# A hybrid decoder layer on one core: the SSM states' pool laid under the logarithms', conv tails turned in a bank of another ring, halves and norm products tied to other steps

## The chip, the cores and the metric

One core of a Trainium2 chip. The kernel is one launch; its time is the device time in microseconds of that launch, the median of several executions. A profile of one execution stands beside it, with its own time.

## The reference

One inference step of a hybrid decoder layer, for a prompt of 512 positions and for 8 samples of 8 new positions each, 576 columns in all, in fp32. D_MODEL is 1024.

```python
def trunk_layer(x, conv_prev, h0, past, p):
    h = x + 0.5 * swiglu(rmsnorm(x, p['ffn1_norm']), ...)          # d_ff 2816
    xn = rmsnorm(h, p['mix_norm'])
    z, xbc, dt_raw, q, k, v, f_raw, g_ssd, g_att = split_combined(xn @ p['w_in'])
    y_ssd, h_new, conv_new = ssd_branch(z, xbc, dt_raw, conv_prev, h0, p)
    q = rmsnorm(q...); k = rmsnorm(k...)                             # per head of 64
    logf = jax.nn.log_sigmoid(f_raw + p['b_f'])
    y_att = fox_attention(q, k_all, v_all, logf_all)                 # past: 2048 paged keys a sample
    merged = (jax.nn.sigmoid(g_ssd) * (y_ssd @ p['w_ssd_proj'])
              + jax.nn.sigmoid(g_att) * (y_att @ p['w_attn_proj']))
    h = h + merged @ p['w_out']
    return h + 0.5 * swiglu(rmsnorm(h, p['ffn2_norm']), ...), (k, v, logf, h_new, conv_new)

def ssd_branch(z, xbc, dt_raw, conv_prev, h0, p):
    xc, conv_new = causal_conv(xbc, conv_prev, ...)                  # 4 taps, SiLU; last 3 rows are an output
    xs, Bm, Cm = jnp.split(xc, ...)                                  # 32 heads of 64; 4 groups of B and C, 128 wide
    y, h_new = ssd_scan(xh, dt, A, Bm, Cm, h0)                       # chunks of 128
    yg = (y + d_skip * xh) * jax.nn.silu(z)
    return yg * lax.rsqrt(mean(yg * yg over a group) + eps) * p['ssd_norm'], h_new, conv_new
```

In a chunk of the scan, y is `(C B^T * decay) @ (x dt)` plus `C` times the state carried in; the state after a chunk is the decayed one plus `B^T` times the decayed `x dt`.

## The kernel before

Activations lie transposed: 128 features on the partitions, the 576 columns along the free axis, worked in two halves of 288. A weight tile of 128x512 comes by DMA from SyncE's queue into `stage`, is rounded by ScalarE into `whi` (L177), and VectorE or GpSimd writes the rest into `wlo` (L178). A product is then three matmuls a tile of 128: hi·hi, hi·lo, lo·hi (`mm3`, L212 to L214), over 128x288. These are called weight matmuls here; a conv tile has 48 of them, a piece of an output product 12.

The text is written for a scheduler (Tile): it fixes for each engine one order of instructions, from the text's order, from priorities (`soon()` puts a few steps ahead) and from ties. `behind(later, first)` is such a tie: it only says that one instruction must not stand before another. Tiles come from pools; a tag has a number of buffers (`bufs`) that are used in turn, and whoever takes one in the text waits until its last user in the text is done. PSUM, which matmuls write, has eight banks: rings of two named `tr`, `mm` and `pv`, and two of `acc`.

In order: the first feed-forward, with side work in between, advanced in steps by a generator (`aside`); the input projection; attention over the pages, with the z part of the projection between (`beside`); then the SSD branch, group by group; the gates, the output projection; the second feed-forward.

What the change touches:

- `aside` loads the rows of the conv state (pool `rows`), then the paged logarithms (pool `lg`): prefix sums, and 32 stores to `pastD` from ScalarE's queue. Then `turns` (pool `turn`, opened after `lg` is closed) loads the 32 tiles of the SSM state (`h`, 256 KB each), turns each with four transposes on TensorE (L390) into a bank `tr`, copies it out and stores it.
- `headnorm` and eight products with `sel8` (L815, two instructions each) spread the q norms' factors over the partitions for the samples; the matmuls of L702 and L786 stand by them. All use 24 partitions.
- In `beside`, a job of z ends with `v = (tanh(v) + 1) * v`, one instruction of VectorE (L1051), and a store to `zD`.
- `conv_tile` makes one of the six tiles of a group (B, C, four of x): two accumulators, moved to `xr` (three buffers, L1154 to L1161); the columns after the prompt are turned (L1167), copied to `tt` (L1169) and stored as outputs; four taps (`kf`, L1178 and L1180), tanh, product (L1182 and L1184). The turned tail goes into the free columns of the second accumulator's own bank, `full`.
- `group_scan(g)` works through the samples' chunk (c = 4) and then the chunks 0 to 3: `cb` (L1312), the log differences `ab` loaded by DMA (L1321), `dk` by ScalarE (relu L1326, exponent L1327) and VectorE (product L1328), x turned (L1337), `xdt` and `xde` (L1342, L1344), then `pv` (L1355, L1359) and the carry of the state (L1370). Samples' parts (`hT`, L1384; `oo`, L1394; L1404) and the last states (L1418, L1420) follow. `halves` writes the gated result in two parts, `ygh` and `ygl` (L1288, L1289).
- `group_in(g + 1)`, the next group's six conv tiles, stands in the text after `group_scan(g)`, and `group_out(g)`, the product with `w_ssd_proj`, after that. `rowscale` (L263 and L265, then small steps of VectorE) gives the norm's factor by which `group_out` scales its accumulators (L1443 to L1446); it takes a bank `tr`.
- The ring `acc` also gives each conv tile's accumulators: `convs` keeps instructions of each tile for ties.

```python
for g in range(4):
    cur = nxt
    *gated, lows = group_scan(g, *cur)
    if g < 3:
        nxt = group_in(g + 1)
        for x in lows[2:4]:
            behind(x, convs[6 * g + 6][3])
    for _ in range((3, 0, 0, 5)[g]):
        j = next(late)
        gate_tile(gs, j, 8 + j)
    if g < 3:
        group_out(g, *gated)
```

Of the kernel before, what the change touches and what calls it, by code (L numbers as in the profile page):

```python
# [23 lines left out]
P = 128  # L24
# [3 lines left out]
NS = 64  # L28
# [65 lines left out]
def build(ctx, tc, A, O):  # L94
# [8 lines left out]
    def pool(name, bufs=1, **kw):  # L103
        return tc.tile_pool(name=name, bufs=bufs, **kw)
# [103 lines left out]
    def mm3(out, w, xs, half, first=True, last=True):  # L208
        n = len(w)
        for i, ((hi, lo), (xh, xl)) in enumerate(zip(w, xs)):  # L210
            a, b = xh[:, hs(half)], xl[:, hs(half)]
            mm(out, lhsT=hi, rhs=a, start=first and i == 0, stop=False)  # L212
            mm(out, lhsT=hi, rhs=b, start=False, stop=False)  # L213
            mm(out, lhsT=lo, rhs=a, start=False, stop=last and i == n - 1)  # L214
# [159 lines left out]
    def turns(wait):  # L374

        for _ in range(wait):
            yield
        with pool("turn", side="right", reuse_waits="tile") as sp_:
            tiles = []
            for t in range(16):  # L380
                for h in range(2):
                    for n in range(len(tiles), min(2 * t + h + 3, 32)):
                        tiles.append(tl(sp_, [P, 4, P], tag="h0", bufs=4))
                        (nc.scalar if n < 3 else nc.sync).dma_start(out=tiles[n], in_=ap3(A["state_ssm"][0], *place(n % 2, n // 2)))
                    if t + h == 0:
                        yield
                    h0 = tiles[2 * t + h]
                    ps = tr()
                    for b in range(4):
                        nc.tensor.transpose(ps[:, b * P:(b + 1) * P], h0[:, b, :], ident)  # L390
                    hT = tl(sp_, [P, 512], tag="hT", bufs=3)
                    act(hT, ps, AF.Copy)
                    nc.scalar.dma_start(out=hTD[h, t], in_=hT)
                    yield

# [27 lines left out]
    with pool("h1", reuse_waits="tile") as hp:  # L423
# [98 lines left out]
        def aside():  # L522

            with pool("rows", side="right", reuse_waits="tile") as su:

                sc = tl(su, [24, CONV], tag="sc")
                for j in range(3):
                    nc.scalar.dma_start(out=sc[j * B:(j + 1) * B], in_=A["state_conv"][0, :, j, :])
                yield
                yield  # L530
                scT = tl(su, [P, 24, 24], tag="scT")
                for j in range(0, 24, 12):
                    t = tr()
                    for i in range(12):
                        nc.tensor.transpose(t[:, i * 24:(i + 1) * 24], sc[:, (j + i) * P:(j + i + 1) * P], ident[:24, :24])
                    V.tensor_copy(scT[:, j:j + 12, :], t[:, :288].rearrange("p (i c) -> p i c", c=24))
                nc.scalar.dma_start(out=scD, in_=scT)

            with pool("lg", side="right", reuse_waits="tile") as lp:
                pcol = tl(lp, [P, 1], I32, tag="pcol")  # L540
                nc.scalar.dma_start(out=pcol, in_=A["page_table"].rearrange("b n -> (b n)").unsqueeze(1))
                lg = tl(lp, [P, P, 16], tag="lg")
                G.indirect_dma_start(out=lg.rearrange("p s h -> p (s h)"), out_offset=None,
                                     in_=A["cache_logf"].rearrange("o n s h -> (o n) (s h)"),
                                     in_offset=bass.IndirectOffsetOnAxis(ap=pcol[:, :1], axis=0))
                pf = tl(lp, [P, 16, P], tag="pf")
                for h in range(16):
                    V.tensor_tensor_scan(pf[:, h, :], C("one"), lg[:, :, h], 0.0, ALU.mult, ALU.add)
                tot = tl(lp, [P, 16], tag="tot")
                V.tensor_copy(tot, pf[:, :, P - 1])  # L550
                page = tl(lp, [P, P], tag="page")
                nc.scalar.dma_start(out=page, in_=A["consts"][:, COFF["page"][0]:COFF["page"][0] + P])
                for _ in range(2):
                    yield
                t = sm()
                mm(t[:, :16], lhsT=page, rhs=tot, start=True, stop=True)
                st = tl(lp, [P, 16], tag="st")
                V.tensor_copy(st, t[:, :16])

                for h in range(16):  # L560
                    G.tensor_tensor(lg.rearrange("p s h -> p (s h)")[:, h * P:(h + 1) * P].rearrange("p (q r u) -> p r q u", q=4, u=4),
                                    pf[:, h, :].rearrange("p (r q u) -> p r q u", q=4, u=4),
                                    st[:, h:h + 1].unsqueeze(2).unsqueeze(3).to_broadcast([P, 8, 4, 4]), ALU.subtract)
                lv = lg.rearrange("p s h -> p (s h)").rearrange("p (h q e) -> p h q e", h=16, q=4)
                for b in range(B):
                    for q in range(4):
                        nc.scalar.dma_start(out=pastD[b, :, q].rearrange("h g e -> g h e"), in_=lv[b * NPG:(b + 1) * NPG, :, q, :])
            yield from turns(1)
# [92 lines left out]
    with pool("att", side="right", reuse_waits="tile") as ap:  # L661
# [147 lines left out]
        G.memset(qz, 0.0)  # L809
        t = sm()  # L810
        for j in range(8):
            sel = sel8[:, j].rearrange("k e m -> k (e m)")
            if j == 0:
                headnorm(qt[0], sel, 64)
            mm(t[:, j * NS:(j + 1) * NS], lhsT=sel, rhs=hr[:, NP:], start=True, stop=True)  # L815
# [211 lines left out]
        def beside():  # L1027
            jobs = [(ga, j) for j in range(8)] + [(zc, j) for j in range(16)]
            ahead = ga.get(0)
            for n, (cols, j) in enumerate(jobs):  # L1030
                w, ahead = ahead, None
                v = tl(mixp, [P, NT], tag="kf", bufs=2)
                for half in range(2):
                    a = acc()
                    for k in range(0, 8, 4):
                        mm3(a, w[k:k + 4], xs[k:k + 4], half, first=k == 0, last=k == 4)
                        if half == 0 and k == 0 and n + 1 < len(jobs):
                            ahead = jobs[n + 1][0].get(jobs[n + 1][1])
                        if k == 0:
                            yield  # L1040
                    with soon():
                        V.scalar_tensor_tensor(v[:, hs(half)], a, 0.5, rbc[:, hs(half)], ALU.mult, ALU.mult)
                    if half == 0:
                        yield
                if cols is ga:
                    act(v, v, AF.Tanh)
                    nc.scalar.dma_start(out=thD[:, j, :], in_=v)
                else:
                    th = tl(tp, [P, NT], tag="sq", bufs=1)
                    act(th, v, AF.Tanh)  # L1050
                    V.scalar_tensor_tensor(v, th, 1.0, v, ALU.add, ALU.mult)  # L1051
                    nc.scalar.dma_start(out=zD[:, j, :], in_=v)
                yield

        filler = beside()
# [26 lines left out]
        for _ in range(24):  # L1082
            fill()
        for n in range(2):
            keys_of(n)
# [58 lines left out]
    def conv_tile(ct, w, prev, out):  # L1144
# [10 lines left out]
        full = tl(accp, [P, 512], tag="acc")  # L1155
        a = full[:, :HT]
# [8 lines left out]
        with soon():  # L1165
            t = full[:n, 512 - P:]
            turned = nc.tensor.transpose(t, xr[:, NP:], ident)  # L1167
            tt = tl(xz, [n, P], tag="tt", bufs=1)
            act(tt, t, AF.Copy)  # L1169
# [37 lines left out]
    with qyp:  # L1207
        with pool("yhl", reuse_waits="tile") as yhp:

            yhl = []  # L1210
            for n, y in enumerate(yt):
# [4 lines left out]
                for x, first in zip((c, h, V.tensor_tensor(lo, y, hi.bitcast(F32), ALU.subtract)), convs[1 + n // 2]):  # L1216
                    behind(x, first)
# [27 lines left out]
    with pool("ssd", side="right", reuse_waits="tile") as wk:  # L1245
# [13 lines left out]
        def group_scan(g, bT, cT, xg):  # L1259
# [8 lines left out]
            yhl, lows, owns = [], [], []  # L1268
# [12 lines left out]
            def halves(half):  # L1281

                for i in range(4):
# [4 lines left out]
                    act(hi, xg[:, i, hs(half)], AF.Copy, scale=w)  # L1288
# [17 lines left out]
            def chunk(c, hst):  # L1306
# [6 lines left out]
                if c == 4:  # L1313
                    behind(cb, convs[6 * g + 2][4])
# [3 lines left out]
                for r0 in (0, 4):  # L1318
# [8 lines left out]
                    act(dv, dv, AF.Exp, scale=-1.0)  # L1327
                    V.tensor_tensor(dv, dv, cbm[:n, :n].unsqueeze(1).to_broadcast([n, 4, n]), ALU.mult)  # L1328
# [60 lines left out]
            for c in range(4):  # L1389
# [5 lines left out]
                if c == 2 and g < 3:  # L1395
                    halves(0)

# [32 lines left out]
            return ysq, yhl, lows  # L1430
# [31 lines left out]
        for g in range(4):  # L1462
            cur = nxt
            *gated, lows = group_scan(g, *cur)
# [90 lines left out]
```

## Time and profile before

| | |
|---|---|
| median of 3 runs | 1868.68 us (1864.07 to 1872.83) |
| profiled execution | 1873.55 us |
| its span | 1871.8 us |
| mean granted clock of TensorE | 0.993 |
| TensorE busy | 1830.4 us |
| VectorE, ScalarE, GpSimd busy | 1060.5, 742.3, 603.2 us |
| read and written in HBM | 223.72 and 38.73 MB |

The span runs from the profile's first instruction to its last; the profiled execution's time has 1.75 us around it. "Busy" counts an engine while an instruction of its own runs, so a matmul at a lower clock counts as longer busy. Idle time is put down to what ended it. The places that the prediction speaks of are the states' loads (at 122 us), the norm products (580), the pages (710 to 813), and the scans of the four groups, whose samples' chunks start near 1000, 1073, 1158 and 1255 us.

### The profile page before, as it was taken

To read this page: it belongs to the slowest core of one execution; us is meant where nothing else is said; L and a number is where in the kernel's file an instruction comes from. 1 tells how busy PE (TensorE), PEld (TensorE's weight loads), DVE (VectorE), ACT (ScalarE), POOL (GpSimd) and SP (SyncE) were. 2 spreads that over 40 slices of the span, in tenths; PEclk is the share of its full clock that TensorE was granted. 3 is DMA by queue.
4 is the path that set the end of the run, shared out by engine and by line. 5 is a ranking of instruction groups with operands and counts; after the bars stand their busy time and mean duration, and the time that the engine had idled before them with its cause. 6 is when DMAs were issued, how large, how long until landed. Compare 5 with 4: busy or idle time off the path is not lost.

```text
span 1871.8 us, 38779 instructions
## 1 busy us (share of the span) xinstructions
PE 1830.4 (98%) x15335; PEld 1727.8 (92%) x15335; DVE 1060.5 (57%) x2297; ACT 742.3 (40%) x1555; POOL 603.2 (32%) x681
## 2 busy tenths in 40 slices
PE   8999999999999999999999999989999999999998
PEld 7999999999889788888998798878999999999998
DVE  4633334433425677876747868787676454344542
ACT  4323223333323555554426555555433333123322
POOL 0423002222321334433324544656553222002210
PEclk9999999999998999999999999999999999999999
DMA  4454443345525678785456545354473444554342
GB/s 149 127 133 127 130 142 102 114 147 158 149 78 159 192 232 240 231 224 158 116 153 183 140 124 140 99 155 137 129 227 91 125 118 127 145 145 123 108 123 64
DMA packets 297722, 269.71 MB, mean 144 GB/s; under 512 B 55068, under 2 KB 262092, under 8 KB 297388
## 3 DMA queue, kind: packets, MB, share of 16 engines
q1 hardware_dynamic: 228128, 183.38, 35.3%
q10 hardware_dynamic: 59412, 46.89, 8.2%
q0 software_dynamic: 10000, 36.97, 6.3%
q8 instruction: 121, 1.98, 0.4%
q14 instruction: 61, 0.50, 0.1%
HBM read 223.72 MB, written 38.73 MB: 140 GB/s over the span
## 4 chain that ended last, share of the span: by engine, by line
PE 64%; DVE 5%; DMA 2%; ACT 1%; issue 1%; POOL 0%; SPq 0%; ACTq 0%; DVEq 0%
PE acc L212 13%; PE acc L214 13%; PE acc L213 13%; PE pv L214 4%; PE pv L212 4%; PE pv L213 4%; PE tr L960 2%; PE tr L947 1%; PE mm L883 1%; PE mm L901 1%; DVE kf L1180 1%; PE pv L1355 1%; PE pv L914 1%; PE mm L1370 1%; PE pv L998 1%
## 5 line engine op out<-in xcount | busy, mean ns | idle before, releaser
L177 ACT ACTIVATE whi<-stage 128x512 fp32r<-128x512 f32 (+2 forms) x474 | 294.3, 622 | 710.5 <-PE acc L213 597.5
L212 PE MATMUL acc<-xh,whi 128*128 128x288 f32 x1792 | 540.9, 302 | 8.8 <-DVE xr L1154 4.8
L213 PE MATMUL acc<-xl,whi 128*128 128x288 f32 x1792 | 532.4, 297 | 0.0
L214 PE MATMUL acc<-xh,wlo 128*128 128x288 f32 x1792 | 532.0, 297 | 0.0
L178 DVE TENSOR_TENSOR wlo<-stage,whi 128x512 fp32r<-128x512 f32 (+1 forms) x373 | 270.4, 725 | 262.3 <-ACT whi L177 246.9
L212 PEld LDWEIGHTS acc<-xh,whi 128*128 128x128 f32 x1792 | 338.5, 189 | 16.1 <-DVE xr L1154 6.6
L213 PEld LDWEIGHTS acc<-xl,whi 128*128 128x128 f32 x1792 | 338.8, 189 | 3.2 <-issue 2.9
L214 PEld LDWEIGHTS acc<-xh,wlo 128*128 128x128 f32 x1792 | 338.2, 189 | 1.3 <-issue 0.8
L178 POOL TENSOR_TENSOR wlo<-stage,whi 128x512 fp32r<-128x512 f32 (+1 forms) x101 | 136.8, 1355 | 277.7 <-ACT whi L177 261.6
L350 POOL TENSOR_TENSOR u<-u,s 128x288 f32<-128x288 f32 x88 | 80.8, 919 | 427.3 <-DVE u L349 371.1
L212 PE MATMUL pv<-xh,whi 128*128 128x288 f32 (+1 forms) x720 | 213.8, 297 | 0.3 <-ACT xh L224 0.3
L213 PE MATMUL pv<-xl,whi 128*128 128x288 f32 (+1 forms) x720 | 212.8, 296 | 0.0
L214 PE MATMUL pv<-xh,wlo 128*128 128x288 f32 (+1 forms) x720 | 212.6, 295 | 0.0
L213 PEld LDWEIGHTS pv<-xl,whi 128*128 128x128 f32 (+1 forms) x720 | 134.7, 187 | 1.2
L212 PEld LDWEIGHTS pv<-xh,whi 128*128 128x128 f32 (+1 forms) x720 | 134.8, 187 | 1.0 <-ACT xh L224 0.6
L214 PEld LDWEIGHTS pv<-xh,wlo 128*128 128x128 f32 (+1 forms) x720 | 134.8, 187 | 0.2
L212 PE MATMUL pv<-hh,whi 128*128 128x288 f32 x352 | 105.9, 301 | 0.0
L352 POOL TENSOR_TENSOR hl<-u,hh 128x288 fp32r<-128x288 f32 x88 | 78.8, 898 | 78.8 <-ACT hh L351 78.8
L212 PE MATMUL acc<-hh,whi 128*128 128x288 f32 x352 | 104.2, 296 | 0.0
L213 PE MATMUL acc<-hl,whi 128*128 128x288 f32 x352 | 104.2, 296 | 0.0
L213 PE MATMUL pv<-hl,whi 128*128 128x288 f32 x352 | 104.1, 296 | 0.0
L214 PE MATMUL acc<-hh,wlo 128*128 128x288 f32 x352 | 104.1, 296 | 0.0
(365 smaller groups left out, 3608.8 us busy)
## 6 DMA issues: line engine op xcount, KB each, us to landing
stage<-in_w_in_dram SPq DMA_DIRECT2D x52, 512.0 KB
stage<-in_ffn_w_up_dram SPq DMA_DIRECT2D x44, 512.0 KB
stage<-in_ffn_w_gate_dram SPq DMA_DIRECT2D x43, 512.0 KB
stage<-in_ffn_w_down_dram SPq DMA_DIRECT2D x40, 512.0 KB
h<-in_state_ssm_dram SPq DMA_DIRECT2D x61, 256.0 KB
hTD<-hT ACTq DMA_DIRECT2D x32, 256.0 KB
pb<-pastD SPq DMA_DIRECT2D x32, 256.0 KB
ab<-cumD SPq DMA_DIRECT2D x32, 256.0 KB
```

Of the source, the lines that this page charges most:

```text
L177: act(hi, view, AF.Copy)
L178: e.tensor_tensor(lo, view, hi.bitcast(F32), ALU.subtract)
L212: mm(out, lhsT=hi, rhs=a, start=first and i == 0, stop=False)
L213: mm(out, lhsT=hi, rhs=b, start=False, stop=False)
L214: mm(out, lhsT=lo, rhs=a, start=False, stop=last and i == n - 1)
L350: G.tensor_tensor(u, u, sil[half], ALU.mult)
L352: G.tensor_tensor(hl[:, hs(half)], u, hh[:, hs(half)].bitcast(F32), ALU.subtract)
L883: mm(s[:, :n], lhsT=q, rhs=ks[2 * self.p + e][:, :n], start=hl == 0, stop=hl == 1)
L901: nc.tensor.transpose(t[:, j * P:(j + 1) * P], lt[:, j * P:(j + 1) * P], ident)
L914: mm(self.ob[o:o + 32, i * P:(i + 1) * P], lhsT=vtok[j][:, v0:v0 + 32], rhs=self.pts[e][:, j * P:(j + 1) * P], start=j == 0, stop=j == i)
L947: nc.tensor.transpose(t[:, i * P:(i + 1) * P], kk[:, i, p * P:(p + 1) * P], ident)
L960: mm(s[kv * 32:(kv + 1) * 32, :], lhsT=self.q(kv), rhs=self.kT[kv // 2], start=True, stop=True)
```

## The change

Line numbers in the rows below are of each kernel's own text; after's are up to 14 higher (L212 to L214 are L213 to L215, L1167 is L1177, L1337 is L1348, L1355 and L1359 are L1366 and L1370).

1. The pool `turn` is opened first and stays beside `rows` and `lg`; all 32 state tiles are loaded from SyncE's queue, the first four early, and the first turn stands before the logarithms' product. The stores to `pastD` go out four a step, each four behind the latest store of a turned state.
2. `conv_tile` turns its tail into a bank `tr()`, and its second half uses `acc()` as the first does.
3. z: ScalarE adds the 1 (Identity with bias), GpSimd multiplies.
4. The eight norm products are tied, two by two, behind pieces of one of the z jobs.
5. Attention's own halves are tied to earlier conv tiles.
6. The samples' chunk's first product is tied behind the tile `6g+3` in place of `6g+2`.
7. The gated halves `ygh` and `ygl` are tied behind chunk 3's exponent and decay of their own scan; the tie of two of them to the next group's first tile is dropped.

```diff
-    def turns(wait):
-        for _ in range(wait):
-            yield
-        with pool("turn", side="right", reuse_waits="tile") as sp_:
+    def turns(sp_, put):
...
-                        (nc.scalar if n < 3 else nc.sync).dma_start(out=tiles[n], in_=...)
+                    nc.sync.dma_start(out=tiles[n], in_=...)
...
-                    nc.scalar.dma_start(out=hTD[h, t], in_=hT)
+                put.append(nc.scalar.dma_start(out=hTD[h, t], in_=hT))
...
         def aside():
-            with pool("rows", side="right", reuse_waits="tile") as su:
+            with pool("turn", side="right", reuse_waits="tile") as tp_:
+                with pool("rows", side="right", reuse_waits="tile") as su:
...
+                    put = []
+                    states = turns(tp_, put)
+                    next(states)
+                    yield
+                    yield next(states)
                     t = sm()
                     mm(t[:, :16], lhsT=page, rhs=tot, start=True, stop=True)
...
                     for b in range(B):
+                        yield next(states)
                         for q in range(4):
-                        nc.scalar.dma_start(out=pastD[...], in_=lv[...])
-            yield from turns(1)
+                            past = nc.scalar.dma_start(out=pastD[...], in_=lv[...])
+                            behind(past, put[-1])
+                yield from states
...
-            mm(t[:, j * NS:(j + 1) * NS], lhsT=sel, rhs=hr[:, NP:], start=True, stop=True)
+            qnorms.append(mm(t[:, j * NS:(j + 1) * NS], lhsT=sel, rhs=hr[:, NP:], start=True, stop=True))
...
-                    V.scalar_tensor_tensor(v, th, 1.0, v, ALU.add, ALU.mult)
+                    act(th, th, AF.Identity, bias=1.0)
+                    G.tensor_tensor(v, th, v, ALU.mult)
...
+        for j in range(8):
+            behind(qnorms[j], pieces[16 + j // 2])
...
-        full = tl(accp, [P, 512], tag="acc")
-        a = full[:, :HT]
+        a = acc()
         mm3(a, w, xs, 1)
...
-            t = full[:n, 512 - P:]
+            t = tr()[:n, :P]
             turned = nc.tensor.transpose(t, xr[:, NP:], ident)
...
-                for x, first in zip((c, h, V.tensor_tensor(lo, y, hi.bitcast(F32), ALU.subtract)), convs[1 + n // 2]):
+                for x, first in zip((c, h, V.tensor_tensor(lo, y, hi.bitcast(F32), ALU.subtract)), convs[1 + 3 * n // 8]):
...
-                    behind(cb, convs[6 * g + 2][4])
+                    behind(cb, convs[6 * g + 3][4])
...
+            for h, l in zip(highs, lows):
+                behind(h, expo[3])
+                behind(l, decay[3])
...
-                for x in lows[2:4]:
-                    behind(x, convs[6 * g + 6][3])
```

Here `pieces[n]` is the last matmul of the n-th run of 12 in `beside`, and `expo[c]`, `decay[c]` are the last instructions of L1327 and L1328 in chunk c.

What this makes of the order. First VectorE in the first scan, around chunk 3. The rows before:

```order
L1328 TENSOR_TENSOR dk_13045<-dk_13045,cbm_13041 128x512
L1154 TENSOR_TENSOR xr_13508<-acc_13511,rbc_5369 128x288
L1289 SCALAR_TENSOR_TENSOR ygl_13024<-xg_11773,P_31_125,ygh_13023 128x288
L1289 SCALAR_TENSOR_TENSOR ygl_13028<-xg_11773,P_31_125,ygh_13027 128x288
L1289 SCALAR_TENSOR_TENSOR ygl_13032<-xg_11773,P_31_125,ygh_13031 128x288
L1289 SCALAR_TENSOR_TENSOR ygl_13036<-xg_11773,P_31_125,ygh_13035 128x288
L1342 TENSOR_TENSOR xdt_13070<-mm_13065,TT_911_5401 128x512
L1344 TENSOR_TENSOR xde_13072<-mm_13065,wdec_12697 128x512
L1328 TENSOR_TENSOR dk_13056<-dk_13056,cbm_13041 128x512
```

and the rows after:

```order
L1339 TENSOR_TENSOR dk_13067<-dk_13067,cbm_13063 128x512
L1339 TENSOR_TENSOR dk_13078<-dk_13078,cbm_13063 128x512
L1353 TENSOR_TENSOR xdt_13092<-mm_13087,TT_911_5401 128x512
L1355 TENSOR_TENSOR xde_13094<-mm_13087,wdec_12719 128x512
L1300 SCALAR_TENSOR_TENSOR ygl_13046<-xg_11791,P_31_125,ygh_13045 128x288
L1300 SCALAR_TENSOR_TENSOR ygl_13050<-xg_11791,P_31_125,ygh_13049 128x288
```

The four halves have moved from before xdt and the second dk to behind them.

TensorE at the end of the same scan. `mm_13065` before and `mm_13087` after are the x of chunk 3 turned; `pv_13078` and `pv_13100` are its products; between the two stood 28 rows of weight matmuls on `acc_13537` and `acc_13590`, of which the last are, before:

```order
L212 MATMUL acc_13590<-xh_5266,whi_13583 128x288
L213 MATMUL acc_13590<-xl_5267,whi_13583 128x288
L214 MATMUL acc_13590<-xh_5266,wlo_13584 128x288
L212 MATMUL acc_13590<-xh_5358,whi_13583 128x288
L1355 MATMUL pv_13078<-dk_13045,xdt_13070 64x128
L1359 MATMUL pv_13078<-ab_13043,hst_13006 64x128
```

After, chunk 3 from its first rows, and then from the last carry to the next weight matmul (the tails are the rows of L1177):

```order
L1381 MATMUL mm_13026<-xde_12992,bt_12996 128x512
L1395 MATMUL pv_13031<-hT_13038,cz_12715 32x128 x2
L1323 MATMUL mm_13061<-cT_11706,bT_11621 128x128
L1418 MATMUL tr_13151<-ident_76,oo_12799 128x128
L1348 MATMUL mm_13087<-ident_76,xg_11791 128x128 x4
L1357 MATMUL mm_13096<-ident_76,bT_11621 128x128
L1366 MATMUL pv_13100<-dk_13067,xdt_13092 64x128
```

```order
L1381 MATMUL mm_13128<-xde_13094,bt_13098 128x512
L1418 MATMUL tr_13151<-ident_76,oo_12799 128x128
L1432 MATMUL tr_13176<-ident_76,hst_13130 128x128 x4
L1177 MATMUL tr_13256<-ident_76,xr_13200 91x128
L1177 MATMUL tr_13341<-ident_76,xr_13285 91x128
L1177 MATMUL tr_13426<-ident_76,xr_13370 91x128
L213 MATMUL acc_13537<-xh_4717,whi_13526 128x288
```

From chunk 2's products to the last of these rows there is no weight matmul; the fifth and sixth tile of the next group (`acc_13537` and later) follow behind three turned tails.

TensorE at the start of the third scan. Before, the last conv tile's tail stands between turned x, and 48 weight matmuls of `group_out(1)` come before the last x of chunk 0:

```order
L1337 MATMUL mm_15491<-ident_76,xg_14761 128x128 x2
L1167 MATMUL acc_15044<-ident_76,xr_15015 91x128
L1337 MATMUL mm_15491<-ident_76,xg_14761 128x128
L1337 MATMUL mm_15432<-ident_76,xg_14761 64x128
L212 MATMUL acc_15132<-ygh_14451,whi_15112 128x288
```

After, two runs of 12 on `acc_15150` and `acc_15166` stand around the tail and the row scale (L265), and behind the second this comes, up to the third run:

```order
L215 MATMUL acc_15166<-ygh_14491,wlo_15147 128x288
L1348 MATMUL mm_15466<-ident_76,xg_14791 64x128
L1323 MATMUL mm_15503<-cT_14706,bT_14621 128x128
L1348 MATMUL mm_15525<-ident_76,xg_14791 128x128 x4
L1348 MATMUL mm_15466<-ident_76,xg_14791 64x128
L1366 MATMUL pv_15489<-dk_15450,xdt_15471 64x64 x4
L1366 MATMUL pv_15489<-dk_15459,xdt_15471 64x64 x4
L1357 MATMUL mm_15534<-ident_76,bT_14621 128x128
L1366 MATMUL pv_15538<-dk_15509,xdt_15530 64x128 x4
L1381 MATMUL mm_15558<-xde_15532,bt_15536 128x512
L1323 MATMUL mm_15576<-cT_14706,bT_14621 128x128
```

Before, this row scale stood some 190 rows ahead of the last tail; now it stands behind it. The fourth scan starts in the same way.

More of the change, by code (lines that the diff above doesn't have):

```diff
@@ L539, in aside @@
[L539 to L553, printed above, removed]
-                    yield
[L555 to L567, printed above, removed]
```

97 lines of the change are left out of this document (63 added, 34 removed).

## The prediction

> **What bounds the kernel now.** I read the page first, then the waits of TensorE, then TensorE's granted clock in small windows, then the timeline where the waits lie. The page:
>
> ```profile
> span 1871.8 us, 38779 instructions
> PE 1830.4 (98%) x15335; PEld 1727.8 (92%) x15335; DVE 1060.5 (57%) x2297; ACT 742.3 (40%) x1555; POOL 603.2 (32%) x681
> ```
>
> TensorE is busy for all but 41 us of the span and no other engine comes near. Matrix work is neither added nor removed, so only two things can move the time: the idle time of TensorE and the clock at which it runs. The view of waits, for TensorE alone (line, releaser: us in total, times, longest):
>
> ```profile
> PE acc L212 <- DVE xr L1154: 4.8, 4, 3.2
> PE pv L1355 <- DVE xdt L1342: 4.7, 3, 2.3
> PE tr L947 <- DVE PTs L989: 3.3, 3, 1.1
> PE tr L390 <- DMA h<-in_state_ssm_dram: 2.7, 1, 2.7
> PE mm L1312 <- DVE cT L1184: 1.7, 1, 1.7
> PE acc L212 <- ACT tt L1169: 1.5, 5, 0.4
> PE acc L212 <- DVE sq L1240: 0.7, 1, 0.7
> PE mm L1370 <- ACT bt L1349: 0.6, 1, 0.6
> PE acc L213 <- DVE yl L1216: 0.4, 1, 0.4
> ```
>
> All nine are at places that the change touches; together they are 20.4 us. The second view is the windows (start:end, length, busy us of each engine with its instructions, then PEclk, the granted clock):
>
> ```profile
> 119.20:122.60 3.40, 0.75 (x7) 0.54 (x7) 3.05 (x5) 2.17 (x6) 1.94 (x2) 1.00 1.02 279
> 122.60:126.10 3.50, 3.50 (x18) 3.50 (x17) 0.64 (x2) 0.60 (x1) 0.48 (x1) 0.53 0.48 157
> 576.70:580.10 3.40, 3.40 (x18) 2.26 (x18) 1.60 (x3) 0.47 (x1) 0.00 (x0) 1.00 0.53 178
> 580.10:590.30 10.20, 10.20 (x40) 8.70 (x40) 9.44 (x26) 3.47 (x7) 2.76 (x5) 0.50 0.55 155
> 1051.60:1058.40 6.80, 6.80 (x41) 3.99 (x41) 6.57 (x14) 3.79 (x12) 2.55 (x6) 0.53 0.57 126
> 1246.00:1249.40 3.40, 3.40 (x10) 2.37 (x11) 3.40 (x7) 0.33 (x2) 1.36 (x2) 0.53 1.05 322
> 1300.00:1303.40 3.40, 3.40 (x41) 3.15 (x39) 2.88 (x8) 1.81 (x4) 3.18 (x3) 1.00 0.57 155
> ```
>
> The reader is to see that a long wait is paid twice. TensorE worked 0.75 of the 3.4 us before 122.6, and then ran 3.5 us at 0.53. The same follows the 3.2 us wait that ends at 1245.9 and the 2.3 us wait that ends at 1049.97 (6.8 us at 0.53). One such stretch has no wait ahead of it, 580.1 to 590.3; its work is this:
>
> ```profile
> 577.69 1.98 PE L702 MATMUL tr<-hr,bias 24*128 24x512 f32 x4
> 579.90 3.36 PE L815 MATMUL mm<-hr,vv 24*128 24x64 f32 x16
> 583.06 2.02 PE L702 MATMUL tr<-hr,vv 24*128 24x512 f32 x2
> ```
>
> These matmuls use 24 rows of the array. TensorE counts as busy throughout, yet the clock halves. What the four stretches cost is length times the missing clock: 1.6, 5.1, 3.2 and 1.6 us, 11.5 us in all.
>
> The Trainium skill (TensorE: Matmul & The Clock Gate, "Part 1: The HAM clock gate") says that the clock is halved after a window of about 3.4 us in which TensorE was idle, and is given back after a busy one. The trace agrees on the half and the 3.4 us. It differs on idle: the stretch at 580 comes after small matmuls without any gap. By the letter of that page of the Trainium skill the move of the norm products would give nothing, and the sum below would be 4 us higher, 1882.
>
> **The change part by part: what it takes away.** States' loads: the wait of 2.7 us on the first state and its cold 1.6 us go, 4.3 us. The first four loads, 256 KB each, now stand on SyncE's queue ahead of a 512 KB weight stage; nothing waits for that stage for tens of us, so I put no cost on it (bound: 0 to 2 us). The 32 stores of the logarithms' prefix leave one block on ScalarE's queue and go out four at a time.
>
> Norm products: sixteen instructions of line 815 leave the block and stand in pairs between weight matmuls. What remains in one place is three L702 and one L786, about 3 us at full clock instead of 5. Between nothing (the clock halves anyway) and 5.1 us; I take 4, since a block under one 3.4 us window can at worst spoil one.
>
> The z gate: one VectorE instruction of line 1051 becomes an addition on ScalarE and a product on GpSimd.
>
> ```profile
> L1051 DVE SCALAR_TENSOR_TENSOR kf<-sq,kf 128x576 f32<-128x576 f32 x16 | 17.5, 1094 | 0.0
> L350 POOL TENSOR_TENSOR u<-u,s 128x288 f32<-128x288 f32 x88 | 80.8, 919 | 427.3 <-DVE u L349 371.1 <-DVE pf L519 45.0 <-DVE s L306 11.0
> ```
>
> VectorE is relieved of 16 x 1.09 us; GpSimd pays about twice L350's 0.92, 1.84 us a time, and ScalarE some 0.7. Both lie beside matmuls. The store of z waits on ScalarE's queue for GpSimd, with exponentials queued behind it, which have microseconds of slack. The three PTs waits follow late VectorE copies: 3.3 us gained (bounds 0 and 3.3).
>
> Turned tails: the 1.5 us on tt go, since the transposes leave the accumulators' banks. Attention's halves tied earlier: yl and sq, 1.1 us, I take 1.0. First product of the samples' chunk one conv tile later: the 1.7 us on cT go.
>
> Gated halves behind chunk 3's exponent and decay: before, they stand in front of them. In the first scan:
>
> ```profile
> 1044.89 0.41 ACT L1326 ACTIVATE dk<-ab,TT 128x128 f32<-128x128 f32 x1 [5.30 <-DMA ab<-cumD]
> 1046.60 1.80 ACT L1288 ACTIVATE ygh<-xg,P 128x288 fp32r<-128x288 f32 x4
> 1048.31 0.61 ACT L1327 ACTIVATE dk<-dk 128x512 f32<-128x512 f32 x1
> 1047.22 2.09 DVE L1289 SCALAR_TENSOR_TENSOR ygl<-xg,P,ygh 128x288 fp32r<-128x288 f32 x4 [2.81 <-ACT ygh L1288]
> 1049.24 0.68 DVE L1342 TENSOR_TENSOR xdt<-mm,TT 128x512 f32<-128x512 f32 x1
> 1049.97 0.45 PE L1355 MATMUL pv<-dk,xdt 128*64 128x128 f32 x4 [2.35 <-DVE xdt L1342]
> ```
>
> VectorE's ygl sit before xdt, TensorE waits 2.35 us. Crediting the old waits there in full: xdt 4.7 and its cold 3.2; xr 4.8 and its cold 1.6; bt 0.6. Of all this I keep back 2.0 for the third scan, whose last chunk has less filler around it than before.
>
> Sum of the gains: 4.3 + 4 + 3.3 + 1.5 + 1.0 + 1.7 + 7.9 + 6.4 + 0.6 - 2.0 = 28.7 us.
>
> **What it adds.** The tails' transposes now take one of the two banks that the scan's own transposes use, and banks go round in the order of the program's text. A conv tile of the next group is written after the scan, so its tail waits for the scan's last state transposes; its input buffer (three in rotation) stays held, and at most four conv tiles run ahead. In the first scan two tiles, 96 weight matmuls, fall behind the scan, and TensorE's order has not one weight matmul between chunk 2 and the tails. What these filled before, by the windows of tile acc, and of all TensorE for the first of them:
>
> ```profile
> 1037.60:1049.90 12.30, 7.67 (x53) 1.00 0.66 177
> 1051.40:1063.10 11.70, 5.91 (x37) 0.72 0.55 143
> 1037.60:1049.90 12.30, 10.03 (x80) 1.00 0.66 177
> 1038.41 0.76 SPq L1321 DMA_DIRECT2D ab<-cumD x1
> 1063.12 0.58 ACT L1420 ACTIVATE x<-tr 128x512 f32<-128x512 f32 x1
> ```
>
> First stretch: 12.3 us, of which TensorE had 10.03 - 7.67 = 2.4 us of other work. Without the detour over ygh and ygl (1048.31 less 1046.2, 2.1 us) the chain from the load of ab at 1038.41 takes 10.2 us; with a load that lands sooner, some 7.5. Idle: 5 to 8, I take 5.5. Second stretch, to the copy of the last states at 1063.12: 11.7 us, at most 5.8 of it other work; the chain (chunk 3, states, their transposes, ScalarE's copy, with the next group's first exponents ahead of it) stays, and ScalarE has less beside it. Idle 3 to 8; I take 5. Then two further tails wait each for a copy on ScalarE, and the next tile's accumulator for VectorE, which has the last step of that group's B ahead of it: 0 to 6, I take 4.5. First scan: 15 us of idle, bounds 8 and 22.
>
> The row scale of the gated norm takes such a bank too, and it too now comes after the last tail. At the starts of the third and fourth scan that leaves two accumulators' worth of output products, 24 matmuls, and then only steps of the new scan, which need the last conv tile. In the fourth, before (the last row is of tile acc again):
>
> ```profile
> 1273.57 0.39 DVE L1159 TENSOR_TENSOR xr<-acc,rbc 128x224 f32<-128x224 f32 x1 [0.35 <-PE acc L214]
> 1281.34 0.83 DVE L1184 SCALAR_TENSOR_TENSOR xg<-xr,kf 128x64 f32<-128x64 f32 x1
> 1282.93 0.38 PE L1337 MATMUL mm<-ident,xg 128*128 128x128 f32 x2
> 1273.50:1282.90 9.40, 8.46 (x62) 1.00 0.31 91
> ```
>
> From the last accumulator to that tile's x are 8.6 us (1282.1 less 1273.5); before, 62 weight matmuls filled them. Now 24 do, some 3.3 us by the same row, with 0.6 of transposes: 4.5 us idle. After it the samples' chunk and chunk 0 follow one another through VectorE (xdt, the row scale's small steps, the second decay) with no filler, about 3.5 us more. 8 us for each start, bounds 3 and 11: 16 us.
>
> Cold clock after these holes, at 1.6 to 1.7 us a window as above: two windows in the first scan, one at each start, 6.8 us (0 to 12). Sum of the losses: 15 + 16 + 6.8 = 37.8 us.
>
> **Sum.** 37.8 - 28.7 = +9.1 us on the profiled execution's 1873.55, 1882.6. That execution lies 4.9 us above the median of the runs, 1868.68, so the forecast is 1877.8, called 1878.
>
> **The rivals.** Faster: the holes are short. If the chains through the last conv tile run quicker without filler's loads beside them, each hole is at its lower bound: 8 + 6 + 1.7 us of cold clock, 15.7 against 28.7, which gives 1856. For it speaks that ScalarE and VectorE each carry less in those stretches; against it, that the chains are made of loads and in-order steps that the filler did not lengthen. It decides where the holes together come to less than 19 us. Chance 0.27.
>
> Even: holes of 24 to 32 us, the first scan at 10 and the starts at 6; 1868, between 1864 and 1872. Chance 0.25. For it: every estimate above is a chain of parts, and parts overlap.
>
> Worse: the holes at their upper bounds and the clock at half through them, 22 + 22 + 12 = 56 us, 1896. For it: the stretch from 1051.6 shows that two windows in a row go cold with light scan matmuls in them. Chance 0.12.
>
> That a part doesn't do what it says: the norm products keep their cold stretch (chance 0.3, since a window of 3.4 us can still fall on the 3 us that remain; 1882 in place of 1878), or the PTs waits come back (0.2; 1881). Either stays inside the cases.
>
> **How the numbers follow.** The forecast case, 1872 to 1888 about 1878, has 0.36. A difference of 0.5%, 9.3 us, is about what this measurement can tell from no change, so its limits are 1859 and 1878. Slower: 0.12 and two thirds of 0.36, 0.36. Faster: the first rival, 0.27. The rest, 0.37, is within. The range that leaves out no more than 2 in 10 runs from the first rival's 1856 to 1892, short of the worst.
>
> **What would show it.** Right: no wait at 122 us, and full clock after it; full clock, or one cold window, near 580; no PTs waits and none on tt; in the first scan a wait on xdt of 5 us, then waits on oo, x and tt of several us with no weight matmul between; at the starts of the third and fourth scan a wait on xg of 4 us and low clock after. Wrong: TensorE's idle time at or under 35 us, or gaps at the starts of scans under 2 us. The prediction fails most easily in the size of these three holes, which no row of before shows.

## The result and the profile after

The changed kernel takes 1878.42 us (median of 8, 1874.24 to 1882.13), the kernel before in the same comparison 1868.88 (8 runs, 1863.1 to 1872.83): 1.0053 times as long, with a 95% interval of 1.0037 to 1.0070, so 7 to 13 us slower. The forecast was 1878. The profiled execution took 1874.24 us, the lowest of its runs; the one profiled before, 1873.55, lies above all eight runs of its kernel. The two spans differ by 0.6 us only, and the medians decide.

The page after:

```profile
span 1872.4 us, 38799 instructions
PE 1832.3 (98%) x15335; PEld 1730.9 (92%) x15335; DVE 1033.9 (55%) x2281; ACT 756.1 (40%) x1571; POOL 623.4 (33%) x697
```

VectorE has sixteen instructions less, ScalarE and GpSimd sixteen more: the z gate. TensorE's idle time is as before, 40 us. What it waited for (line, releaser: us in total, times, longest):

```profile
PE pv L1366 <- DVE xdt L1353: 7.2, 5, 2.6
...
PE acc L213 <- DVE sq L1250: 3.2, 1, 3.2
PE mm L1348 <- DVE xg L1192: 3.0, 2, 1.5
PE acc L213 <- DVE xr L1165: 2.6, 3, 1.8
PE mm L1348 <- DVE cbm L1327: 2.4, 2, 1.2
PE tr L1177 <- ACT x L1434: 2.2, 1, 2.2
```

The waits on the first state, on PTs and on cT are gone, that on tt has shrunk to 0.3 us. In their place stand waits on xg and cbm, one of each at either start, of the third and of the fourth scan; on x, in front of the tails at the end of the first scan; on sq, in the middle of attention's projection. The windows, for TensorE alone (start:end, length, busy us and instructions, granted clock, DMA share, GB/s):

```profile
1034.10:1037.50 3.40, 3.40 (x35) 0.53 0.71 141
1044.50:1051.50 7.00, 5.19 (x21) 0.51 0.44 114
1177.40:1181.10 3.70, 1.09 (x7) 1.00 0.01 2
1181.10:1187.40 6.30, 6.16 (x49) 0.50 0.30 85
1174.00:1190.00 16.00, 12.33 (x89) 0.79 0.33 104
1270.00:1286.00 16.00, 12.26 (x85) 0.68 0.44 129
```

The reader is to see the holes and the cold clock behind them: 1.09 us of work in 3.7, then 6.3 us at half clock. The end of the first scan, where the order shows no weight matmul:

```profile
1034.08 0.54 PE L1366 MATMUL pv<-dk,xdt 128*64 128x128 f32 x4 [2.31 <-DVE xdt L1353]
1040.66 0.66 PE L1432 MATMUL tr<-ident,hst 128*128 128x128 f32 x4 [0.74 <-DVE hst L1387]
1043.78 0.35 PE L1177 MATMUL tr<-ident,xr 128*91 128x128 f32 x1 [2.18 <-ACT x L1434]
1044.46 0.47 PE L1177 MATMUL tr<-ident,xr 128*91 128x128 f32 x1 [0.34 <-ACT tt L1179]
```

With the 1.8 us on xr that follow, 7.4 us of waits.

The chain ahead of chunk 3's xdt, in the same scan: what SyncE's queue waits for between 1020 and 1036 us, the load of ab, ScalarE's wait for it, VectorE's decays and xdt.

```profile
SPq L1332 <- PE pv L1370: 8.8, 3, 5.9
1026.57 0.37 SPq L1332 DMA_DIRECT2D ab<-cumD  x1
1030.29 1.28 ACT L1337 ACTIVATE dk<-ab,TT 128x128 f32<-128x128 f32 x4 [3.91 <-DMA ab<-cumD]
1031.28 2.15 DVE L1339 TENSOR_TENSOR dk<-dk,cbm 128x512 f32<-128x512 f32 x2
1033.35 0.68 DVE L1353 TENSOR_TENSOR xdt<-mm,TT 128x512 f32<-128x512 f32 x1
```

### The profile page after: what moved, and what is told of

The parts are those of the page before. It is cut to its first block, busy times and chain, and to the rows that moved or that the text cites. A ratio compares the mean times of both kernels' runs of the same rounds, so it can differ in the third digit from the quotient of the medians.

```text
span 1872.4 us, 38799 instructions
## 1 busy us (share of the span) xinstructions
PE 1832.3 (98%) x15335; PEld 1730.9 (92%) x15335; DVE 1033.9 (55%) x2281; ACT 756.1 (40%) x1571; POOL 623.4 (33%) x697
## 3 DMA queue, kind: packets, MB, share of 16 engines
q8 instruction: 121, 1.98, 0.4%
## 4 chain that ended last, share of the span: by engine, by line
PE 85%; DMA 4%; DVE 4%; POOL 3%; ACT 2%; issue 2%; SPq 0%; ACTq 0%; DVEq 0%; POOLq 0%
PE acc L213 16%; PE acc L215 16%; PE acc L214 16%; PE pv L214 8%; PE pv L213 8%; PE pv L215 8%; PE tr L966 2%; DMA ab<-cumD 1%; PE tr L953 1%; PE mm L889 1%; DVE kf L1190 1%; PE pv L920 1%; PE mm L907 1%; PE pv L1004 1%; PE tr L389 1%
## 5 line engine op out<-in xcount | busy, mean ns | idle before, releaser
L213 PE MATMUL acc<-xh,whi 128*128 128x288 f32 x1792 | 540.3, 302 | 3.4 <-DVE xr L1165 2.6
L215 PE MATMUL acc<-xh,wlo 128*128 128x288 f32 x1792 | 531.7, 297 | 0.0
L214 PE MATMUL acc<-xl,whi 128*128 128x288 f32 x1792 | 531.0, 296 | 0.0
L213 PEld LDWEIGHTS acc<-xh,whi 128*128 128x128 f32 x1792 | 338.3, 189 | 6.9 <-DVE xr L1165 2.7
L215 PEld LDWEIGHTS acc<-xh,wlo 128*128 128x128 f32 x1792 | 337.8, 189 | 2.0 <-issue 1.4
L214 PEld LDWEIGHTS acc<-xl,whi 128*128 128x128 f32 x1792 | 338.3, 189 | 1.4 <-issue 1.1
L213 PE MATMUL pv<-xh,whi 128*128 128x288 f32 (+1 forms) x720 | 214.0, 298 | 0.0
L214 PE MATMUL pv<-xl,whi 128*128 128x288 f32 (+1 forms) x720 | 212.5, 295 | 0.0
L215 PE MATMUL pv<-xh,wlo 128*128 128x288 f32 (+1 forms) x720 | 212.2, 295 | 0.0
L214 PEld LDWEIGHTS pv<-xl,whi 128*128 128x128 f32 (+1 forms) x720 | 134.6, 187 | 1.2
L213 PEld LDWEIGHTS pv<-xh,whi 128*128 128x128 f32 (+1 forms) x720 | 134.8, 187 | 0.7 <-ACT xh L226 0.3
L215 PEld LDWEIGHTS pv<-xh,wlo 128*128 128x128 f32 (+1 forms) x720 | 134.6, 187 | 0.2
L213 PE MATMUL pv<-hh,whi 128*128 128x288 f32 x352 | 105.8, 300 | 0.0
L214 PE MATMUL acc<-hl,whi 128*128 128x288 f32 x352 | 104.2, 296 | 0.0
L214 PE MATMUL pv<-hl,whi 128*128 128x288 f32 x352 | 104.2, 296 | 0.0
L213 PE MATMUL acc<-hh,whi 128*128 128x288 f32 x352 | 104.2, 296 | 0.0
L215 PE MATMUL acc<-hh,wlo 128*128 128x288 f32 x352 | 104.2, 296 | 0.0
L215 PE MATMUL pv<-hh,wlo 128*128 128x288 f32 x352 | 103.8, 295 | 0.0
```

Of the source, the lines that this page charges most:

```text
L215: end = mm(out, lhsT=lo, rhs=a, start=False, stop=last and i == n - 1)
```

## The experiments

The theory was that the tails' bank opens these holes and costs more than all other parts give. The main rivals were that the loss comes from another part, and that waits only move. Each median stands beside that of the kernel before in its own comparison, 1867.9 to 1868.5; intervals are 95%. A difference between two changed kernels, such as a part's cost, comes from two comparisons and is by these intervals good to some 3 or 4 us.

**1. Tails back.** From the changed kernel:

```diff
-        a = acc()
+        full = tl(accp, [P, 512], tag="acc")
+        a = full[:, :HT]
...
-            t = tr()[:n, :P]
+            t = full[:n, 512 - P:]
```

> The changed kernel with the turned tails put back into the accumulators' own banks, everything else kept. Theory: the tails' bank alone opens the three stretches without weight matmuls; in the trace of the changed kernel they hold 10.7 us of waits at the end of the first scan, 3.5 us at the starts of the third and fourth, and some 10 to 13 us of halved clock around them. Undoing it brings these back, less 1.5 us on tt: about 1853 us, between 1848 and 1860. Rival: the waits only move, and the loss comes from the other parts: 1872 to 1880.

1864.95 us, 0.9978 of before (0.9963 to 0.9994). The three holes go, and the part costs 13.5 us. So the direction held, but it is 12 us short of what was expected, since old waits come back:

```profile
PE acc L213 <- DVE xr L1165: 5.4, 5, 3.2
...
PE acc L213 <- ACT tt L1180: 3.7, 8, 1.2
PE acc L213 <- DVE sq L1251: 1.8, 1, 1.8
PE pv L1367 <- DVE xdt L1354: 1.7, 3, 0.7
```

xr and tt now hold 9.1 us. What the tails' bank had spared was more than the 1.5 us on tt, and xr's 4.8 us of before return in full, though the gated halves are still tied. It also says that all the other parts together are worth some 2.9 us (1 to 7).

**2. Tails alone.** In the kernel before:

```diff
-        full = tl(accp, [P, 512], tag="acc")
-        a = full[:, :HT]
+        a = acc()
...
-            t = full[:n, 512 - P:]
+            t = tr()[:n, :P]
```

> The kernel before with the tails' bank moved, nothing else. Theory: the same three stretches appear in the kernel before: 20 to 28 us slower, 1889 to 1897, with no weight matmul between chunk 2 and the tails of the first scan. Rival: the tails' bank is worth its 1.5 us on tt and no more: 1866 to 1869.

1879.60 us, 1.0060 (1.0043 to 1.0078): 11.7 us slower. The holes appear, in the kernel before too:

```profile
PE pv L1354 <- DVE xdt L1341: 7.6, 5, 3.0
PE tr L390 <- DMA h<-in_state_ssm_dram: 4.8, 1, 4.8
PE mm L1336 <- DVE xg L1181: 4.5, 2, 3.0
```

Half of what was expected. Done alone and undone alone, the part costs 11.7 and 13.5 us. That settles where most of the loss comes from. The 3.2 us wait on xr is gone here as well: the list has 2.5 us on xr, at most 1.8 at a time.

**3. Row scale in another ring.** From the changed kernel, tails left as they are:

```diff
     def rowscale(s, inv, r, first=None):
         with soon():
-            t = tr()
+            t = sm()
```

> The changed kernel with the row scale's sums in a bank of the ring mm in place of tr, everything else kept, the tails' bank too. Theory: the row scale, held up behind the last tail, is what leaves the starts of the third and fourth scan with only 24 weight matmuls; with it free, the 3.5 us of waits at each of the two starts and the 3.4 and 5 us that their halved clock costs go: about 1866, between 1862 and 1870. The hole at the end of the first scan stays. Rival: the starts wait for the last conv tile whatever stands beside: 1875 to 1880.

1870.70 us, 1.0016 (1.0008 to 1.0025), 7.7 us under the changed kernel. The two starts again, in this kernel:

```profile
1174.00:1190.00 16.00, 14.36 (x119) 1.00 0.23 62
1270.00:1286.00 16.00, 15.03 (x122) 1.00 0.40 118
```

Full clock and 119 and 122 matmuls in windows that held 89 and 85. So the starts wait because the row scale stands behind the last tail, not for the conv tile as such: output products now fill that wait. This one line takes back 7.7 of the 13.5 us, 4.7 us less than expected. The holes at the end of the first scan are still in this kernel, with 3.2 us on xdt; what they cost by themselves was not tried.

**4. Attention's tie back.** From the changed kernel:

```diff
-                for x, first in zip((c, h, ...), convs[1 + 3 * n // 8]):
+                for x, first in zip((c, h, ...), convs[1 + n // 2]):
```

> The changed kernel with the tie of attention's halves as before. Theory: that tie brought the new wait of 3.2 us at 938 us and the 3.4 us of halved clock after it; without it 1878.4 - 3.2 - 1.7 + 1.1 = about 1874.5. Rival: the wait is that of a load (kf from thD) which comes late for a reason of its own, a buffer kf that conv tiles hold: it stays, 1878.

1874.57 us, 1.0038 (1.0025 to 1.0051); the two intervals overlap, so the 3.9 us rest on the trace as well. The stretch that has the wait on sq, in the changed kernel and then in this one:

```profile
936.00:944.00 8.00, 5.71 (x32) 0.79 0.47 143
```

```profile
936.00:944.00 8.00, 7.50 (x56) 1.00 0.35 111
```

The cold window goes and the wait falls from 3.2 to 1.8 us. VectorE's own wait there is for a load in both (changed kernel, then this one):

```profile
937.68 0.82 DVE L1250 SCALAR_TENSOR_TENSOR sq<-kf,acc 128x288 f32<-128x288 f32 x2 [2.31 <-DMA kf<-thD]
```

```profile
936.00 0.82 DVE L1250 SCALAR_TENSOR_TENSOR sq<-kf,acc 128x288 f32<-128x288 f32 x2 [0.86 <-DMA kf<-thD]
```

The load is late in either kernel, so both theories may have a part. How much of the 3.9 us is the tie's is not settled: over all profiles the longest wait on sq is 1.8 to 3.6 us in the four with the earlier tie and 0.7 to 2.7 in the ten with the old one, and tails_only, with the old one, has its 2.7 and a cold window behind it too.

**5. Norm products alone.** In the kernel before:

```diff
+            qnorms.append(mm(t[:, j * NS:(j + 1) * NS], lhsT=sel, rhs=hr[:, NP:], start=True, stop=True))
...
+        for j in range(8):
+            behind(qnorms[j], pieces[16 + j // 2])
```

> The kernel before with the eight norm products tied behind pieces, nothing else. Theory: the block of matmuls with 24 rows sets the clock back for 10.2 us at 580; broken up it costs no cold window or one: full clock from 580 to 590 and 3.4 to 5.1 us gained, 1864 to 1865.5. Rival: a block of some 3 us is left, and the clock halves as before; or the clock there has another cause: 1868.9.

1866.22 us, 0.9986 (0.9973 to 0.9999): faster, by some 2 us in place of 4. The window of 16 us at this place, of the kernel before in its two profiles and then of this kernel:

```profile
576.00:592.00 16.00, 16.00 (x74) 0.68 0.51 154
```

```profile
576.00:592.00 16.00, 16.00 (x100) 0.89 0.64 183
```

```profile
576.00:592.00 16.00, 16.00 (x106) 1.00 0.62 183
```

The cause is right, and its size came from one execution: the same program loses 5.1 us there (0.32 of 16) in one execution and 1.8 (0.11) in the next.

**6. States' pool alone.** In the kernel before, part 1 of the change:

```diff
-                        (nc.scalar if n < 3 else nc.sync).dma_start(out=tiles[n], in_=...)
+                    nc.sync.dma_start(out=tiles[n], in_=...)
...
+            with pool("turn", side="right", reuse_waits="tile") as tp_:
```

> The kernel before with the states' pool laid under the others and loaded ahead, nothing else. Theory: the first state's wait goes (2.7 us in the trace of before, 4.8 and 3.7 in two other kernels with the same part) and one window of halved clock behind it, 1.6 us: 4.3 to 6 us gained, about 1863. Rival: the early loads and the spread stores only move the wait to weights: 1868.

1860.93 us, 0.9964 (0.9951 to 0.9977), 7.6 us faster, at the good end of what was expected and beyond. The wait on the first state is not in its list of waits at all.

**7. z gate alone.** In the kernel before:

```diff
-                    V.scalar_tensor_tensor(v, th, 1.0, v, ALU.add, ALU.mult)
+                    act(th, th, AF.Identity, bias=1.0)
+                    G.tensor_tensor(v, th, v, ALU.mult)
```

> The kernel before with the z gate's product on GpSimd and the addition on ScalarE, nothing else. Theory: the three PTs waits of 1.1 us go: 3.3 us gained, 1864.5. Rival: VectorE is on time but the next link, ScalarE's copy kT, is then late by as much: 1867 to 1868.

1870.18 us, 1.0012 (1.0002 to 1.0022): slower, by 0.4 to 4 us. Its waits between 600 and 880 us, and those of the second profile of the kernel before:

```profile
PE tr L960 <- ACT kT L949: 1.3, 4, 0.6
PE tr L947 <- ACT kT L949: 0.7, 1, 0.7
```

```profile
PE tr L947 <- DVE PTs L989: 0.8, 1, 0.8
PE tr L947 <- ACT kT L949: 0.7, 1, 0.7
```

The rival holds: the wait moves to ScalarE's copies. And the three PTs waits of the prediction are one in the second profile: they were of that execution. The stretch from the first to the last of these transposes (L947, 256 of them) lasts 256.8 us against 254.6 there; the waits explain half a microsecond of that, the rest stays open.

**8. Gated halves alone.** In the kernel before:

```diff
+            for h, l in zip(highs, lows):
+                behind(h, expo[3])
+                behind(l, decay[3])
...
-                for x in lows[2:4]:
-                    behind(x, convs[6 * g + 6][3])
```

> The kernel before with the gated halves tied behind chunk 3's exponent and decay, nothing else. Theory: in the first scan the wait of 2.35 us on xdt and the 6.8 us of halved clock behind it go, in the third most of 1.75 and 0.6: 6 to 8 us gained, about 1861. [...]

1865.98 us, 0.9991 (0.9981 to 1.0001): 2.5 us faster, not told from no change. In the first scan of this kernel:

```profile
1035.47 0.76 SPq L1322 DMA_DIRECT2D ab<-cumD  x1
1041.91 0.40 ACT L1327 ACTIVATE dk<-ab,TT 128x128 f32<-128x128 f32 x1 [5.26 <-DMA ab<-cumD]
1044.27 0.81 DVE L1329 TENSOR_TENSOR dk<-dk,cbm 128x512 f32<-128x512 f32 x1 [2.80 <-ACT dk L1328]
1045.00 1.13 DVE L1290 SCALAR_TENSOR_TENSOR ygl<-xg,P,ygh 128x288 fp32r<-128x288 f32 x2
1046.06 0.68 DVE L1343 TENSOR_TENSOR xdt<-mm,TT 128x512 f32<-128x512 f32 x1
```

The theory's 6 to 8 us did not come, and the wait stays. The load of ab, issued at 1035.47, lets ScalarE go on only at 1041.91; the second decay, now ahead of xdt, waits for it, and two halves still pass in front. TensorE waits 2.0 us on xdt there as against 2.35. The half clock behind it is gone (full from 1040 to 1060 us), but that is not the tie's doing for certain: in z_only, without the tie, ScalarE waits 2.9 us for the same load in place of 5.3, TensorE 0.5 us on xdt, and the clock is full too.

**9. Three parts.** States' pool, norm products and gated halves in the kernel before: the edits of 6, 5 and 8.

> The kernel before with three parts of the change: states' pool, norm products, gated halves. Theory (parts add up): their single gains, 7.6, 2.0 and 2.5 us, sum to 12 us, about 1856.5, between 1854 and 1859. Rival: they overlap, since each spares windows of halved clock that fall by chance: 8 us, 1860.

1861.16 us, 0.9961 (0.9947 to 0.9975): 7.3 us faster. The gains don't add to 12; the three give together (5 to 10) what the states' pool gives alone. Why was not tried.

**10. Tails in the ring only where they starve nothing.** On top of 9:

```diff
-                    behind(cb, convs[6 * g + 2][4])
+                    behind(cb, convs[6 * g + 3][4])
...
+        late_g = (ct // 4 if ct < 16 else ct % 4) > 1
+        full = None if late_g else tl(accp, [P, 512], tag="acc")
+        a = acc() if late_g else full[:, :HT]
...
+            t = tr()[:n, :P] if late_g else full[:n, 512 - P:]
...
-            t = tr()
+            t = sm()
             m1 = mm(t, lhsT=C("one"), rhs=s[:, :NP], start=True, stop=True)
```

> three_parts with, on top, the samples' chunk one tile later, the tails in the ring tr for the third and fourth group alone (the first and second keep theirs in the accumulators' banks) and the row scale's sums in the ring mm. Theory: the tails' bank does good where no scan is starved by it: the wait of 3.2 us at 1235 us and the two windows of halved clock behind it go, and no hole opens: 5 us under three_parts. Rival: small waits on the tails and on the row scale take as much: the same as three_parts, within 2 us.

1859.94 us, 0.9950 (0.9932 to 0.9969), the fastest median of all. Against 9 it is 1.2 us, which the two intervals don't tell apart, so the rival holds: the waits on xr that 9 still has (3.9 us, at most 2.3 at a time) are gone, and others of some 2 us each, such as these, have come:

```profile
PE acc L213 <- DVE kf L597: 2.2, 2, 1.4
PE acc L213 <- DVE u L1460: 2.2, 5, 0.7
```

**11 and 12. Both kernels once more**, for a second profile.

> The kernel before once more, for a second profile. Theory: the free-running window of the clock and the loads' luck move the cold stretches from one execution to the next: the 10.2 us at 580 and the 6.8 us at 1052 are not there in the same length, and the three PTs waits are fewer. Rival: they stand as they did, to within 1 us.

> The changed kernel once more, for a second profile. Theory: the holes at the end of the first scan (some 10 us) and at the starts of the third and fourth (3.5 us each) stand as they did, since the order makes them; the cold windows behind them differ in length. Rival: the holes vary as much as the clock does.

1867.76 and 1875.17 us. The kernel before:

```profile
PE acc L212 <- DVE xr L1154: 4.8, 4, 3.2
...
PE pv L1355 <- DVE xdt L1342: 4.1, 3, 2.2
PE tr L390 <- DMA h<-in_state_ssm_dram: 4.1, 1, 4.1
```

and the changed one:

```profile
PE pv L1366 <- DVE xdt L1353: 7.0, 5, 2.5
...
PE acc L213 <- DVE sq L1250: 3.6, 1, 3.6
PE mm L1348 <- DVE xg L1192: 3.0, 2, 1.5
PE acc L213 <- DVE xr L1165: 2.9, 3, 1.9
PE mm L1348 <- DVE cbm L1327: 2.4, 2, 1.2
PE tr L1177 <- ACT x L1434: 2.4, 1, 2.4
```

Waits that the order makes come back to within 0.4 us: xr 4.8 and 4.8; xg 3.0 and 3.0, cbm 2.4 and 2.4, x 2.2 and 2.4. Waits on loads, PTs and the cold stretches don't: the first state 2.7 and 4.1, PTs 3.3 and 0.8, the clock at 580 as shown; nor does the old wait on xdt, which hangs on the load of ab (4.7 and 4.1, and 0.5 in z_only).

## Why the prediction was right, and what in it was wrong

The time and the mechanism of the loss came out, and both sums behind them were too large by about the same amount. The prediction set xr's 6.4 us down to the gated halves; but with the halves alone xr still holds 4.8 us, 3.2 at a time, and with the tails alone that wait is gone, so it belongs to the tails. By the terms, then, the tails' bank should have cost 37.8 us less the 1.5 on tt and the 6.4 on xr and its cold clock, 29.9 us net; undone it measured 13.5, alone 11.7. The other parts should have given 28.7 less those 7.9, 20.8 us; without the tails the kernel gained 2.9. The errors, some 16 and 18 us, cancel: the first alone would have given 1862, the second alone 1896. That 1878 was hit so closely is luck.

- **Holes in the first scan**, 15 us: the place and all three stretches are right, the size is 7.4 us from chunk 3 on. In the first stretch (2.3 us for 5.5) the step that failed is "2.4 us of other work": the load of ab waits for chunk 2's products and goes out at 1026.57, when their first half is done. From there to the end of xdt at 1034.0 the chain takes 7.5 us, as forecast for a load that lands sooner; but TensorE has 5.2 us of work in it, the second half, the carry and what follows up to 1031.8, in part at half clock. The second stretch holds 2.9 us for 5, the third 2.2 for 4.5; why they are short was not tried. A wait of 2.6 us on xdt stands one chunk earlier, where none was forecast.
- **Holes at the two starts**, 8 us each: right in place and cause (experiment 3), but the waits are 1.2, 1.5 and 0.8 us. The forecast 3.5 us for VectorE's small steps are not waited for: TensorE ran the new scan's own matmuls at half clock over them, 6.16 us busy of 6.3. Together the two starts cost 7.7 us by experiment 3, not 19.
- **Cold clock**, 6.8 us (0 to 12): by the prediction's measure, length times missing clock, it is some 15 us, above the bound: 6.8 in the first scan (cold from 1024.2, 1034.1 and 1044.5 us), 3.4 and 5.1 at the starts. But that measure is not what it costs. Over the whole span the changed kernel lacks 17.0 us of clock and the one with the tails back 5.2, while TensorE is busy 4.6 us longer (1832.3 and 1827.7). Holes and cold clock were counted one after the other where they overlap.
- **States' loads**, 4.3 us: 7.6 measured (4 to 9). The wait of 2.7 us was a short one; other profiles with the same loads show 3.7 to 4.8.
- **Norm products**, 4 us: about 2. Cause right, the size taken from one execution. The letter of the page in the Trainium skill (TensorE: Matmul & The Clock Gate, "Part 1: The HAM clock gate"), no gain because TensorE is never idle there, is not what the runs show: the clock is full in six of eight profiles once the small matmuls are spread (experiment 5), and in none of six before.
- **z gate**, 3.3 us: wrong in sign. The lower bound was 0 and should have been below it.
- **Attention's tie**, 1.0 us gained: up to 4 lost, not settled (experiment 4). Tying earlier was read as removing a wait on yl; the load of th, which TensorE then waits for, was not looked at.
- **Gated halves**, 7.9 and 0.6 less 2.0: 2.5, not told from nothing. The step that failed is the credit "in full": taking the detour away leaves the load behind it as the last to end, and xr's wait was never theirs. The tie of cb was not tried alone; its wait of 1.7 us is not in the trace after.
- **Rivals and signs.** "Faster" had its condition met and not its time: the holes come to some 17 us (10 in the first scan, 3.5 at each start), under its 19, but the gains were not there to take the kernel to 1856. One sign of being wrong was met to the letter as well: each gap at the starts is under 2 us, though three of them stand there. TensorE's idle time, 40 us, was not at the 35 that the other sign names, and no wait on oo came.

## What to carry to other kernels

A step that takes a buffer from a ring stands, in that ring, where the program's text puts it; before a tile is moved from a bank of its own into a ring shared with a later stage, list who takes from the ring in between, and which work fills the engine until then. One line that moves the row scale to another ring was worth as much as the best part of the change (7.7 and 7.6 us). Take a gain from one profile only if the order makes the wait; a wait on a load, or a cold stretch, should be seen in a second profile first.

## What the runs showed of the hardware

A block of small matmuls on 24 rows set the clock back, though TensorE shows busy 16.00 us of 16; whether their rows, their few columns or their number decide was not tried. In eight profiles with the norm products tied, six have full clock there and two one window of 3.4 us; in the six without, all have one to three windows (mean clock of the 16 us: 0.68, 0.79, and 0.89 four times). So one program loses 1.8 to 5.1 us at one place from execution to execution: 3.3 of the 5.8 us between the two profiled executions of the kernel before.

The length of a wait alone does not tell whether the clock falls behind it: after 2.03 us on xdt in the first scan of states_only it is at 0.50 to 0.58 from 1043 to 1046 us, after 1.98 us at the same place in halves_only it stays full.
